# A new opening for a two-layer hybrid block: first shift and scale ahead of x, x in halves, first weights split in slices

## Chip, cores and metric

The kernel runs on one core of one Trainium2 chip. The metric is the device time of one execution in microseconds. Engines are named as in the profile: PE is TensorE, DVE is VectorE, ACT is ScalarE, POOL is GpSimd, SP is SyncE, whose queue issues the transfers (DMAs) here.

## The reference, cut to what matters

Two layers run over 256 latent tokens (x) and 256 context tokens (ctx), 1024 features wide, in fp32. The opening of a layer is a normalisation with a shift and a scale that come from a vector c, followed by one combined input product:

```python
mod = (jax.nn.silu(c) @ w_mod[l] + b_mod[l])[:, None, :]
sh1, sc1, gt1, sh2, sc2, gt2 = jnp.split(mod, N_MOD, axis=-1)
h = rms_norm(x, g_norm1[l]) * (1 + sc1) + sh1      # the same for ctx with c_ctx
z = h @ w_in[l]                                    # 1024 x 4864
# z's columns: conv gates B, C, X (256 each), Fourier F (256), q, k, v, three gates
y_conv = z_B * conv3(z_C * z_X);  y_four = Re(FFT2(z_F));  y_attn = attention(q, k, v)
x = x + gt1 * (gated sum of the three branches @ w_o)
x = x + gt2 * (relu(h2 @ w_ff1) ** 2 @ w_ff2)      # h2: normalised and modulated again
```

The second layer gives the latent tokens only.

## The kernel before

Activations lie feature-major: 128 features of one feature tile on the partitions, 512 tokens (two streams of 256) in the free dimension; there are eight feature tiles (`KT = 8`). For accuracy every product is made of three passes: each operand is split into a high part (`hi`, a rounded copy made by ACT, line 356) and a low part (`lo`, the difference, line 357). In `fm` the passes are lines 416 (high x high), 419 (low weight x high) and 421 (high weight x low activation). A product of one feature tile with the three first weight chunks (F, C, X of `w_in`, 256 columns each) is thus 18 matmuls of 512 columns.

The program is written for a scheduler that orders the instructions of each engine ahead of time by its own model; `tc.keep_in_program_order` pins an instruction behind the one written before it on its engine. Engines then execute their streams strictly in order, and so does SP's queue of transfers. A tile of a pool with n buffers can be written only when the n-th tile before it has been read for the last time. What matters here: `rpool` has two raw weight tiles (1 MB each); the first two weight chunks take both, the third chunk takes the two `modr` tiles, and the next users of the raw tiles are the conv weights (`convL_raw`, columns B of `w_in`) and the Fourier tables (`fouL_raw`).

The opening of layer 0 goes as follows.

- SP issues c and c_ctx, x, ctx (one transfer of 1 MB each), four small row tables (`load_rows`), and then the shift and scale columns of `w_mod` for the eight feature tiles (`start_mod`, line 447, 16 transfers of 512 KB), with the three first weight chunks in two halves of 512 KB each (`start_weights`, line 461), the first halves after the very first `w_mod` part, the second halves after four feature tiles.
- ACT squares x and ctx (line 474), GpSimd raises to the power -1/2 (line 171), VectorE and TensorE spread the result over the partitions (lines 191, 192). TensorE transposes x and ctx (line 480), VectorE and ACT copy the result (line 484).
- For each feature tile, `mod_start` multiplies the `w_mod` columns with silu(c) on TensorE (line 245), VectorE copies the sums (line 252), TensorE turns them (line 254; called the turn of a tile below), VectorE adds the bias (lines 258, 262) and makes the gain (line 231). `modulate` makes the two streams of the tile: VectorE line 209, ACT line 214 (the high part), VectorE line 201 (the low part). The products of the tile before stand around it on TensorE.
- The weight chunks are split in halves of 1024 columns (`Chunk.prep`); of the six low parts four are made by GpSimd (`G`) and two by VectorE.
- Afterwards come the conv stage (products with columns B), Fourier mixing, and q, k, v. Small tables for q and k (`gqk`, `ropec`, `ropes`) are fetched behind the opening's transfers and prepared by VectorE at lines 648 to 654; these instructions are not pinned and the scheduler places them.

Of the kernel before, what the change touches and what calls it, by code (L numbers as in the profile page):

```python
# [15 lines left out]
P = 128  # L16
# [9 lines left out]

# How the streams of work are interleaved in program order.
TAIL = 2                        # low-part passes left for after the next group's start
CT = 4                          # feature tiles of the context's modulation per turn
HEAD = 4                        # feature tiles of stream 0 modulated ahead of stream 1  # L30
NT0 = 2
MLAG = 1                        # tiles between a modulated tile and its split
LAG = 2                         # tiles between a product and its residual
W1, W2 = 3, 2
RATES = [0.6, 1.3, 0.4, 0.8]    # background work emitted per tick
AR = [1.3, 0.8]                 # attention work emitted per tick


@with_exitstack
def hybrid_block_kernel(  # L40
# [30 lines left out]
    def bigt(shape, dt=F32R):  # L71
        return big.tile(shape, dt, tag="big", name=nm("big"))
# [23 lines left out]

# [1 line left out]
    rows = [scratch((P, P)) for _ in range(DEPTH)]  # L98
# [9 lines left out]
    nc.sync.dma_start(crow[8:16, :], c_ctx.rearrange("(a b) -> a b", b=P))  # L108
    xraw = bigt([P, 2, 2, D], F32)
    for i, src in enumerate((x[0], ctx_in[0])):  # L110
        nc.sync.dma_start(xraw[:, i], src.rearrange("(t p) d -> p t d", p=P))
    load_rows(0)

# [30 lines left out]

# [1 line left out]
    xT = const.tile([P, KT, 2 * S], F32, tag="xT", name="xT")  # L146
# [27 lines left out]
    def spread(acc):  # L174
        """1 / rms of each token, on every partition."""
        nt = acc.n // P
        ssp = aux((P, 4))
        for src in (acc.t, acc.q):
            for tt in range(nt):
                PE.matmul(  # L180
                    ssp[:, tt : tt + 1], src[:, tt * P : (tt + 1) * P], ones[:, 0:1],
                    start=src is acc.t and tt == 0, stop=src is acc.q and tt == nt - 1,
                )
        return spread_rows(ssp[:, :nt], nt)[:, : acc.n]
# [38 lines left out]

# [1 line left out]
    modT = [const.tile([P, 48, 2], F32, tag=f"modT{l}", name=f"modT{l}") for l in range(DEPTH)]  # L225
# [11 lines left out]

    def mod_start(ft, parts, meanwhile):
        """Shift and scale of one feature tile, the sums over even and odd k side by side."""
        pb = pmod.tile([P, 2, P], F32, tag="mod", name=nm("mod"))  # L240
        ps, tp = pb[:, 0, :], pb[:, 1, :]
        for kt in range(KT):
            for i in range(2):
                g = 2 * i + kt % 2
                mm = PE.matmul(
                    ps[32 * g : 32 * g + 32, :], cT[:, kt, :], parts[:, i, kt, :],
                    start=kt < 2, stop=kt >= KT - 2,
                )
                if ft and kt == 0 and i == 0:
                    tc.keep_in_program_order(mm)  # L250
        sb = scratch()[:, :P]
        V.tensor_copy(sb, ps)
        meanwhile()
        tc.keep_in_program_order(PE.transpose(tp, sb, ident))
        tv = tp.rearrange("p (g s) -> p g s", s=32)
        for i in (1, 0):
            m = modT[0][:, i * 8 + ft, :]
            V.tensor_tensor(
                m, tv[:, 2 * i, 0:2], prm[0][:, i * 8 + ft : i * 8 + ft + 1].to_broadcast([P, 2]),
                op=ALU.add,  # L260
            )
            V.tensor_tensor(m, tv[:, 2 * i + 1, 0:2], m, op=ALU.add)

# [10 lines left out]
    def mod_finish(accs, dsts, l):  # L274
        """Sum each of two accumulators over the partitions into a column of four features."""
        ps = pmod.tile([P, 256], F32, tag="mod", name=nm("mod"))
# [54 lines left out]

# [1 line left out]
    class Side:  # L333
# [17 lines left out]

# [1 line left out]
    def split(src, n, pin=False, eng=V):  # L353
# [9 lines left out]
    class Chunk:  # L363
# [9 lines left out]
        def at(self, kt, c0, n):  # L373
            hi, lo = self.pieces[kt // 4]
            o = (kt % 4) * 256 + c0
            return hi[:, o : o + n], lo[:, o : o + n]

    def fetch(loads, nkt=8, eng=(V, V)):
        r = raw_tile()
        for dst, src in loads(r.rearrange("p (k n) -> p k n", n=256)):  # L380
            nc.sync.dma_start(dst, src)
        return Chunk([r[:, i * 1024 : (i + 1) * 1024] for i in range(nkt // 4)], eng=eng)
# [10 lines left out]
    def fm(chunks, src, cols, banks=None, kts=range(8), first=None, final=None, pin=False,  # L393
           turn=False, tail=0):
        """Feature-major product. turn: one output tile after the other; tail: so many of the
        last k tiles go chunk after chunk."""
        kts = list(kts)
# [42 lines left out]

# [1 line left out]
    def start_mod(q):  # L442
        t = bigt([P, 2, 2, KT, P], F32)
        for f in range(2):
            for i in (1, 0):
                c0 = i * D + (2 * q + f) * P
                nc.sync.dma_start(  # L447
                    t[:, f, i], w_mod[0, :, c0 : c0 + P].rearrange("(k p) n -> p k n", p=P)
                )
                if (q, f, i) == (0, 0, 0):  # L450
                    start_weights(0)
        return t

# [11 lines left out]

    sc0 = [start_mod(0), start_mod(1)]
    start_weights(1)
    sc0 += [start_mod(2), start_mod(3)]
    first_w = [Chunk(r, True, e) for r, e in zip(start_raw, ((G, V), (G, G), (V, G)))]

# [18 lines left out]

# [1 line left out]
    for l in range(DEPTH):  # L491
# [5 lines left out]

        # modulated norm, Fourier input and the convolution's first factor
        stage[0] = f"n1L{l}"
        sh1 = modT[l][:, 0:8, :]  # L500
        if l == 0:
            hh, hl = bigt([P, KT, 512]), bigt([P, KT, 512])
            gn = None
        else:
            gn = gain(l, 1, 48)
# [4 lines left out]
        if l == 0:  # L510
            banks = [bank() for _ in range(4)] + [aux() for _ in range(2)]

            def go(kt, a=0, b=3):
                fm(first_w[a:b], hsrc, (0, T), banks[2 * a : 2 * b], (kt,), 0, 7, True)

            first_w[0].prep(0)

            def between(kt):
                if kt > 1:
                    go(kt - 1, 0, 1)  # L520
                if kt == KT // 2:
                    first_w[1].prep(1)

            for kt in range(KT):
                mod_start(kt, sc0[kt // 2][:, kt % 2], lambda: between(kt))
                gn = gain(0, 1, 48, gn, kt, 1)
                modulate(hh, hl, [(kt, 0), (kt, 1)], rb, gn, sh1)
                if kt == 0:
                    for w in first_w[1:]:
                        w.prep(0)  # L530
                    turn_x(range(NT0, KT))
                    go(0, 0, 1)
                if kt:
                    go(kt - 1, 1, 3)
                if kt in (2, 4):
                    first_w[kt - 2].prep(1)
            for i in range(3):
                go(KT - 1, i, i + 1)
            mods.set(mod_steps(
                [(0, j, 2) for j in range(2, 6)] + [(1, 1, 2), (1, 0, 2)]  # L540
                + [(1, j, 1) for j in range(2, 6)]
            ), 0.0)
        else:
            banks = fm(first_w, hsrc, (0, T), tail=TAIL)
            banks = banks[2:] + banks[:2]
# [18 lines left out]

        # gated short convolution
        stage[0] = f"convL{l}"
# [34 lines left out]

        # Fourier mixing, over channels
        stage[0] = f"fouL{l}"
# [23 lines left out]

        # Fourier mixing, over positions
        stage[0] = f"fouL{l}"
# [11 lines left out]

        # queries, keys and values, token-major
        stage[0] = f"qkvL{l}"
# [111 lines left out]

        # attention, in steps between the gate products
        ar = Ring(8)
# [64 lines left out]

        # gates and branch projections
        stage[0] = f"gateL{l}"
# [64 lines left out]
        def project(get, src, gt, acc, spreads):  # L889
            """x += gt * (src @ w); the last two chunks go stream by stream when two streams run."""  # L890
            lag = ns == 2 and acc is not None
# [31 lines left out]
        def early(ft):  # L923
            """x times the gain; the product with w_ff1 is divided by the rms instead of x."""
            xf, g = xT[:, ft, :T], gn2[:, ft, 0:1]
# [14 lines left out]

        # MLP
        stage[0] = f"ffL{l}"
# [140 lines left out]
```

## Time and profile before

| | us |
|---|---|
| median of 3 runs | 1157.92 |
| lowest and highest run | 1157.07, 1158.3 |
| span of the profiled execution | 1156.9 |
| busy in it: PE, DVE, ACT, POOL | 1134.0, 781.5, 501.3, 59.3 |

The profile page gives no other time of the profiled execution than its span; the runs shown lie 0.2 to 1.4 us above it. A row of the timeline gives start, duration, engine, line of the kernel, operation, output and inputs, and how often it came in a row; in brackets stands how long the engine had been idle before it and what ended that. Rows that the profile counts as `x2` are two instructions taken together. A matmul's duration overlaps with the next one's, so the pace is read from the starts.

### The profile page before, as it was taken

How to read it: one execution, taken by the hardware profiler on the slowest of the kernel's cores; microseconds unless marked ns; L12 is line 12 of the kernel's file. 1: busy time of each engine (PE TensorE's matmuls, PEld its weight loads, DVE VectorE, ACT ScalarE, POOL GpSimd, SP SyncE). 2: the span in 40 equal slices, each digit the busy share in tenths (PEclk: the TensorE clock that was granted, in tenths of full speed). 3: DMA queues.
4: the chain of work that ended last, by engine and by line, in shares of the span. 5: the costliest groups of instructions: out<-in, count | busy, mean ns of one | idle time of the engine just before them, and what ended most of it. 6: DMA issues, size and time to landing. Idle time of an engine off the chain costs nothing.

```text
span 1156.9 us, 18548 instructions
## 1 busy us (share of the span) xinstructions
PE 1134.0 (98%) x7451; PEld 1001.1 (87%) x7451; DVE 781.5 (68%) x1446; ACT 501.3 (43%) x890; POOL 59.3 (5%) x57
## 2 busy tenths in 40 slices
PE   6899999999999999999999999999999999999998
PEld 4689987887787998878888888899999999999998
DVE  4677775567879785776746664678876567755754
ACT  4244444434332454144234135244666456744641
POOL 2102100000000100000000000043300000000000
PEclk9999999999999999999999999999999999999999
DMA  9923222234656253555455664515434465555552
GB/s 289 288 80 107 92 91 92 83 90 120 192 167 189 77 175 129 185 181 180 134 176 199 212 211 150 188 63 182 129 129 127 123 209 172 197 183 176 189 187 81
DMA packets 165743, 180.06 MB, mean 156 GB/s; under 512 B 5245, under 2 KB 144153, under 8 KB 165657
## 3 DMA queue, kind: packets, MB, share of 16 engines
q1 hardware_dynamic: 165656, 178.88, 49.1%
q8 instruction: 58, 0.95, 0.3%
q14 instruction: 29, 0.23, 0.1%
HBM read 177.81 MB, written 1.05 MB: 155 GB/s over the span
## 4 chain that ended last, share of the span: by engine, by line
PE 90%; SPq 3%; DMA 3%; DVE 2%; ACT 1%; POOL 0%; issue 0%; DVEq 0%; ACTq 0%
PE ffL_mm L416 15%; PE ffL_mm L419 14%; PE ffL_mm L421 14%; PE gateL_mm L416 5%; PE gateL_mm L419 5%; PE gateL_mm L421 5%; PE agL_mm L416 3%; PE agL_mm L419 3%; PE agL_mm L421 3%; SPq L447 2%; PE woL_mm L419 2%; PE woL_mm L421 2%; PE woL_mm L416 2%; PE gateL_aux L796 2%; PE gateL_aux L771 2%; PE qkvL_mm L748 2%
## 5 line engine op out<-in xcount | busy, mean ns | idle before, releaser
L356 ACT CAST ffL_whi<-ffL_raw 128x1024 fp32r<-128x1024 f32 x128 | 134.2, 1050 | 223.5 <-PE ffL_mm L421 211.4
L357 DVE TENSOR_TENSOR ffL_wlo<-ffL_raw,ffL_whi 128x1024 fp32r<-128x1024 f32 x127 | 155.2, 1223 | 102.7 <-ACT ffL_whi L356 102.6
L416 PE MATMUL ffL_mm<-ffL_big,ffL_whi 128*128 128x256 f32 (+1 forms) x544 | 173.3, 329 | 0.3 <-DVE xT L434 0.3
L419 PE MATMUL ffL_mm<-ffL_big,ffL_wlo 128*128 128x256 f32 (+1 forms) x544 | 172.3, 327 | 0.0
L416 PE MATMUL ffL_mm<-woL_big,ffL_whi 128*128 128x258 f32 (+2 forms) x544 | 171.2, 328 | 0.0
L419 PE MATMUL ffL_mm<-woL_big,ffL_wlo 128*128 128x258 f32 (+2 forms) x544 | 170.8, 327 | 0.0
L421 PE MATMUL ffL_mm<-ffL_big,ffL_whi 128*128 128x256 f32 (+1 forms) x544 | 137.9, 327 | 0.0
L421 PE MATMUL ffL_mm<-woL_big,ffL_whi 128*128 128x258 f32 (+2 forms) x544 | 134.0, 328 | 0.0
L416 PEld LDWEIGHTS ffL_mm<-ffL_big,ffL_whi 128*128 128x128 f32 x544 | 103.4, 190 | 11.0 <-issue 2.5
L416 PEld LDWEIGHTS ffL_mm<-woL_big,ffL_whi 128*128 128x128 f32 x544 | 102.7, 189 | 10.2 <-issue 1.6
L419 PEld LDWEIGHTS ffL_mm<-ffL_big,ffL_wlo 128*128 128x128 f32 x544 | 103.4, 190 | 9.0 <-issue 0.4
L419 PEld LDWEIGHTS ffL_mm<-woL_big,ffL_wlo 128*128 128x128 f32 x544 | 102.9, 190 | 8.9 <-issue 0.4
L323 DVE SCALAR_TENSOR_TENSOR ffL_acc<-ffL_modr,cs,ffL_acc 128x512 f32<-128x512 f32 x126 | 90.4, 747 | 25.9 <-DMA ffL_modr<-in_w_mod_dram 24.8
L421 PEld LDWEIGHTS ffL_mm<-ffL_big,ffL_whi 128*128 128x128 f32 x544 | 93.6, 190 | 8.6
L421 PEld LDWEIGHTS ffL_mm<-woL_big,ffL_whi 128*128 128x128 f32 x544 | 91.2, 189 | 8.7
L357 DVE TENSOR_TENSOR gateL_wlo<-gateL_raw,gateL_whi 128x1024 fp32r<-128x1024 f32 x40 | 48.9, 1222 | 13.4 <-ACT gateL_whi L356 13.3
L356 ACT CAST gateL_whi<-gateL_raw 128x1024 fp32r<-128x1024 f32 x40 | 42.0, 1050 | 26.9 <-PE gateL_mm L421 20.7
L774 DVE TENSOR_REDUCE gateL_mx<-gateL_aux 128x1 f32<-128x512 f32 (+1 forms) x48 | 28.7, 600 | 34.5 <-PE gateL_aux L771 34.2
L434 DVE SCALAR_TENSOR_TENSOR xT<-ffL_mm,modT,xT 128x256 f32<-128x256 f32 x80 | 34.1, 478 | 25.3 <-PE ffL_mm L421 25.2
L416 PE MATMUL gateL_mm<-n1L_big,gateL_whi 128*128 128x512 f32 x128 | 50.8, 398 | 0.0
L419 PE MATMUL gateL_mm<-n1L_big,gateL_wlo 128*128 128x512 f32 x128 | 50.8, 397 | 0.0
L419 PE MATMUL woL_mm<-agL_big,woL_wlo 128*128 128x256 f32 (+1 forms) x160 | 47.4, 307 | 0.0
(325 smaller groups left out, 2447.6 us busy)
## 6 DMA issues: line engine op xcount, KB each, us to landing
ffL_raw<-in_w_ff_dram SPq DMA_DIRECT2D x64, 1024.0 KB, 5.2
ffL_modr<-in_w_mod_dram SPq DMA_DIRECT2D x53, 512.0 KB, 5.6
gateL_raw<-in_w_in_dram SPq DMA_DIRECT2D x16, 1024.0 KB, 7.1
init_big<-in_w_mod_dram SPq DMA_DIRECT2D x16, 512.0 KB, 7.6
agL_raw<-in_w_in_dram SPq DMA_DIRECT2D x8, 1024.0 KB, 5.2
woL_raw<-in_w_o_dram SPq DMA_DIRECT2D x8, 1024.0 KB
qkvL_raw<-in_w_in_dram SPq DMA_DIRECT2D x6, 1024.0 KB
agL_modr<-in_w_mod_dram SPq DMA_DIRECT2D x11, 512.0 KB, 3.6
```

Source lines behind the costliest of these rows:

```text
L323: v = V.scalar_tensor_tensor(a, r[:, kk, :], w, a, op0=ALU.mult, op1=ALU.add)
L356: a = A.copy(hi[:, :n], src)
L357: b = eng.tensor_tensor(lo[:, :n], src, hi[:, :n].bitcast(F32), op=ALU.subtract)
L416: m = PE.matmul(d, wh, rh, start=kt == first, stop=False)
L419: PE.matmul(d, wl, rh, start=False, stop=False)
L421: PE.matmul(d, wh, rl, start=False, stop=kt == final)
L434: V.scalar_tensor_tensor(xT[:, f, cs], ps[:, cs], gt[:, f, s : s + 1], xT[:, f, cs], op0=ALU.mult, op1=ALU.add,)
L447: nc.sync.dma_start(t[:, f, i], w_mod[0, :, c0 : c0 + P].rearrange("(k p) n -> p k n", p=P))
L748: PE.matmul(ps, a, wh, start=kt == 0, stop=False)
L771: PE.matmul(sc, qT[:, h, q0 : q0 + P], kT[:, h // 4, e, ks], start=e == 0, stop=e == 1)
L774: V.reduce_max(mx, sc, axis=AX.X, negate=True)
L796: PE.matmul(yp[g * HD : (g + 1) * HD, :], vt[:, k0 + kk, g * HD : (g + 1) * HD], pts[g][:, kk, :], start=kk == 0, stop=kk == nk - 1,)
```

## The change

What it does:

- the `w_mod` columns of feature tile 0 are fetched directly after c, then the row tables, and x and ctx behind them, each in two halves of 512 KB; `mod_start(0)` and its gain stand ahead of the squares;
- `mod_start` takes one or two feature tiles and all its TensorE and VectorE instructions are pinned; tiles 4 and 5 are taken together;
- the first weight chunks (`Sliced`) are split slice by slice: 256 columns of each chunk per feature tile, high part on ACT, low part on VectorE, pinned behind the modulation of the tile; GpSimd makes none;
- the second halves of the weights are fetched after six feature tiles instead of four;
- products come in another order: those of tile 0 with the first two chunks stand ahead of `mod_start(1)`, and for the pair 4 and 5 all products of tile 4 stand ahead of `mod_start(6)`.

```diff
+    def start_mod(t, f):
+        for i in (1, 0):
+            c0 = i * D + f * P
+            nc.sync.dma_start(
+                t[:, f % 2, i], w_mod[0, :, c0 : c0 + P].rearrange("(k p) n -> p k n", p=P)
+            )
+
+    sc0 = [bigt([P, 2, 2, KT, P], F32)]
+    start_mod(sc0[0], 0)
+    load_rows(0)
     for i, src in enumerate((x[0], ctx_in[0])):
-        nc.sync.dma_start(xraw[:, i], src.rearrange("(t p) d -> p t d", p=P))
-    load_rows(0)
+        for tt in range(2):
+            nc.sync.dma_start(xraw[:, i, tt], src[tt * P : (tt + 1) * P, :])
...
-    def mod_start(ft, parts, meanwhile):
+    def mod_start(f0, parts, meanwhile):
+        n = parts.shape[1]
+        pb = pmod.tile([P, 2, n, P], F32, tag="mod", name=nm("mod"))
+        ps, tp = pb[:, 0], pb[:, 1]
         for kt in range(KT):
             for i in range(2):
                 g = 2 * i + kt % 2
+                tc.keep_in_program_order(PE.matmul(
+                    ps[32 * g : 32 * g + 32], cT[:, kt, :], parts[:, :, i, kt, :],
                     start=kt < 2, stop=kt >= KT - 2,
+                ))
+        sb = scratch((P, 4, P))[:, :n]
+        tc.keep_in_program_order(V.tensor_copy(sb, ps))
         meanwhile()
+        for f in range(n):
+            tc.keep_in_program_order(PE.transpose(tp[:, f], sb[:, f], ident))
...
+    class Sliced(Chunk):
+        def part(self, k0, k1):
+            i = k0 // 4
+            if i not in self.pieces:
+                self.pieces[i] = [wpool.tile([P, 1024], F32R, tag=t, name=nm(t))
+                                  for t in ("whi", "wlo")]
+            hi, lo = self.pieces[i]
+            c = slice((k0 - 4 * i) * 256, (k1 - 4 * i) * 256)
+            tc.keep_in_program_order(A.copy(hi[:, c], self.raws[i][:, c]))
+            tc.keep_in_program_order(V.tensor_tensor(
+                lo[:, c], self.raws[i][:, c], hi[:, c].bitcast(F32), op=ALU.subtract))
...
-    sc0 = [start_mod(0), start_mod(1)]
-    start_weights(1)
-    sc0 += [start_mod(2), start_mod(3)]
-    first_w = [Chunk(r, True, e) for r, e in zip(start_raw, ((G, V), (G, G), (V, G)))]
+    start_weights(0)
+    for f in range(1, KT):
+        if f % 2 == 0:
+            sc0.append(bigt([P, 2, 2, KT, P], F32))
+        start_mod(sc0[f // 2], f)
+        if f == 5:
+            start_weights(1)
+    first_w = [Sliced(r) for r in start_raw]
+
+    mod_start(0, sc0[0][:, 0:1], lambda: None)
+    gn = gain(0, 1, 48, None, 0, 1)
...
-            for kt in range(KT):
-                mod_start(kt, sc0[kt // 2][:, kt % 2], lambda: between(kt))
-                gn = gain(0, 1, 48, gn, kt, 1)
-                modulate(hh, hl, [(kt, 0), (kt, 1)], rb, gn, sh1)
...
+            groups = [(0,), (1,), (2,), (3,), (4, 5), (6,), (7,)]
+            due = []
+            for n, fts in enumerate(groups):
+                while len(due) > 1:
+                    go(due.pop(0))
+                f0, nf = fts[0], len(fts)
+                cut = 2 if n == 1 else 1
+                if n == 1:
+                    go(0, 0, 2)
+                if n:
+                    mod_start(f0, sc0[f0 // 2][:, f0 % 2 : f0 % 2 + nf],
+                              lambda: n == 1 or go(due[0], 0, 1))
+                    gn = gain(0, 1, 48, gn, f0, nf)
+                else:
+                    first_w[0].part(0, 1)
+                modulate(hh, hl, [(f, s) for f in fts for s in range(2)], rb, gn, sh1)
+                for w in first_w[not n :]:
+                    w.part(f0, f0 + nf)
+                if n == 0:
                     turn_x(range(NT0, KT))
+                else:
+                    go(due.pop(0), cut, 3)
+                due += fts
             for i in range(3):
                 go(KT - 1, i, i + 1)
```

More of the change, by code (lines that the diff above doesn't have):

```diff
@@ L236, in gain @@
         return g
-    def mod_start(ft, parts, meanwhile):
-        pb = pmod.tile([P, 2, P], F32, tag="mod", name=nm("mod"))
-        ps, tp = pb[:, 0, :], pb[:, 1, :]
+    def mod_start(f0, parts, meanwhile):
+        n = parts.shape[1]
+        pb = pmod.tile([P, 2, n, P], F32, tag="mod", name=nm("mod"))
+        ps, tp = pb[:, 0], pb[:, 1]
         for kt in range(KT):
@@ L244, in mod_start @@
                 g = 2 * i + kt % 2
-                mm = PE.matmul(
-                    ps[32 * g : 32 * g + 32, :], cT[:, kt, :], parts[:, i, kt, :],
+                tc.keep_in_program_order(PE.matmul(
+                    ps[32 * g : 32 * g + 32], cT[:, kt, :], parts[:, :, i, kt, :],
                     start=kt < 2, stop=kt >= KT - 2,
[L248 to L252, printed above, removed]
+                ))
+        sb = scratch((P, 4, P))[:, :n]
+        tc.keep_in_program_order(V.tensor_copy(sb, ps))
         meanwhile()
-        tc.keep_in_program_order(PE.transpose(tp, sb, ident))
-        tv = tp.rearrange("p (g s) -> p g s", s=32)
+        for f in range(n):
+            tc.keep_in_program_order(PE.transpose(tp[:, f], sb[:, f], ident))
+        tv = tp.rearrange("p f (g s) -> p f g s", s=32)
         for i in (1, 0):
-            m = modT[0][:, i * 8 + ft, :]
-            V.tensor_tensor(
-                m, tv[:, 2 * i, 0:2], prm[0][:, i * 8 + ft : i * 8 + ft + 1].to_broadcast([P, 2]),
+            a = i * 8 + f0
+            m = modT[0][:, a : a + n, :]
+            tc.keep_in_program_order(V.tensor_tensor(
+                m, tv[:, :, 2 * i, 0:2], prm[0][:, a : a + n].unsqueeze(2).to_broadcast([P, n, 2]),
                 op=ALU.add,
-            )
-            V.tensor_tensor(m, tv[:, 2 * i + 1, 0:2], m, op=ALU.add)
+            ))
+            tc.keep_in_program_order(
+                V.tensor_tensor(m, tv[:, :, 2 * i + 1, 0:2], m, op=ALU.add))
     def mod_loads(todo):
@@ L376, in at @@
             return hi[:, o : o + n], lo[:, o : o + n]
+    class Sliced(Chunk):
[7 more added lines that the diff above has]
+            tc.keep_in_program_order(A.copy(hi[:, c], self.raws[i][:, c]))
+            tc.keep_in_program_order(V.tensor_tensor(
+                lo[:, c], self.raws[i][:, c], hi[:, c].bitcast(F32), op=ALU.subtract))
     def fetch(loads, nkt=8, eng=(V, V)):
@@ L439, in residual @@
                 acc[s].add(f)
[L442 to L452, printed above, removed]
     start_raw = [raw_tile(), raw_tile()]
@@ L502, in hybrid_block_kernel @@
             hh, hl = bigt([P, KT, 512]), bigt([P, KT, 512])
-            gn = None
         else:
@@ L514, in go @@
                 fm(first_w[a:b], hsrc, (0, T), banks[2 * a : 2 * b], (kt,), 0, 7, True)
[L516 to L522, printed above, removed]
-            for kt in range(KT):
-                mod_start(kt, sc0[kt // 2][:, kt % 2], lambda: between(kt))
-                gn = gain(0, 1, 48, gn, kt, 1)
-                modulate(hh, hl, [(kt, 0), (kt, 1)], rb, gn, sh1)
-                if kt == 0:
-                    for w in first_w[1:]:
-                        w.prep(0)
-                    turn_x(range(NT0, KT))
[L532 to L536, printed above, removed]
+            groups = [(0,), (1,), (2,), (3,), (4, 5), (6,), (7,)]
[17 more added lines that the diff above has]
+                if n == 0:
+                    turn_x(range(NT0, KT))
+                else:
+                    go(due.pop(0), cut, 3)
+                due += fts
             for i in range(3):
```

## The prediction

> **What bounds the kernel now.** I read the page first, then the windows of the opening, then the timeline engine by engine.
>
> ```profile
> span 1156.9 us, 18548 instructions
> ...
> PE   6899999999999999999999999999999999999998
> ...
> PEclk9999999999999999999999999999999999999999
> DMA  9923222234656253555455664515434465555552
> ...
> PE 90%; SPq 3%; DMA 3%; DVE 2%; ACT 1%; POOL 0%; issue 0%; DVEq 0%; ACTq 0%
> ...
> L357 DVE TENSOR_TENSOR ffL_wlo<-ffL_raw,ffL_whi 128x1024 fp32r<-128x1024 f32 x127 | 155.2, 1223 | 102.7 <-ACT ffL_whi L356 102.6
> ```
>
> The chain that ended last is 90% TensorE. Apart from the last slice, only the first two of the 40 have TensorE below 9 and they alone have full transfers, so a change to the opening can win only there. The L357 row prices a whole split on VectorE at 1.22 us. The next view cuts the opening at events used below (us; busy time and count of each engine; granted clock, DMA share, GB/s).
>
> ```profile
> 7.16:20.19 13.03, 9.21 (x74) 7.88 (x74) 6.79 (x20) 8.49 (x16) 3.38 (x2) 1.00 1.11 325
> 20.19:27.87 7.68, 7.17 (x51) 5.07 (x52) 5.53 (x13) 2.74 (x4) 2.37 (x1) 0.78 1.15 292
> 27.87:44.27 16.40, 16.40 (x154) 12.54 (x154) 9.04 (x30) 5.02 (x9) 1.57 (x1) 1.00 1.12 302
> 44.27:54.97 10.70, 7.55 (x53) 5.16 (x52) 7.77 (x26) 1.66 (x3) 3.35 (x2) 0.84 0.94 268
> 54.97:69.66 14.69, 14.69 (x121) 11.73 (x120) 8.09 (x24) 5.39 (x10) 0.27 (x4) 1.00 0.18 62
> 70.00:80.00 10.00, 10.00 (x48) 8.27 (x47) 7.95 (x13) 2.45 (x4) 0.00 (x0) 1.00 0.67 215
> 790.00:795.00 5.00, 3.74 (x32) 3.54 (x31) 5.00 (x11) 2.53 (x4) 0.92 (x2) 1.00 0.65 208
> ```
>
> TensorE idles 3.8 us before 20.19 (13.03 less 9.21) and 3.2 us in 44.27:54.97. After each idle stretch the clock is below 1, which costs (1 - 0.78) x 7.68 = 1.7 us and (1 - 0.84) x 10.70 = 1.7 us: one cold spell is 1.7 us. Between and after, it never idles; the conv stage from 69.66 finds its weights ready. So the measure is when that stage can start, 69.66 now. These rows carry the two stalls and the pace:
>
> ```profile
> 9.93 1.06 ACT L474 ACTIVATE init_junk<-init_big 128x1024 fp32r<-128x1024 f32 x1 [0.60 <-DMA init_big<-in_ctx_dram]
> ...
> 11.93 0.19 ACT L474 ACTIVATION_READ_ACCUMULATOR init_junk<-init_big 128x1 f32 x1
> ...
> 12.59 1.02 POOL L171 TENSOR_TENSOR init_rstd<-init_var,mhalf 128x4 f32<-128x4 f32 x1 [10.78 <-DVE init_var L169]
> ...
> 13.65 0.88 DVE L191 TENSOR_SCALAR init_scr<-ident,init_rstd 128x128 f32<-128x128 f32 x4
> ...
> 18.72 0.87 DVE L209 SCALAR_TENSOR_TENSOR n1L_scr<-xT,n1L_gain,init_aux 128x256 f32<-128x256 f32 x2
> ...
> 20.19 0.80 PE L416 MATMUL n1L_mm<-n1L_big,n1L_whi 128*128 128x512 f32 x1 [2.99 <-ACT n1L_big L214]
> ...
> 24.86 0.33 PE L254 MATMUL n1L_mod<-ident,n1L_scr 128*128 128x128 f32 x1 [0.50 <-DVE n1L_scr L252]
> ...
> 38.80 1.08 PE L245 MATMUL n1L_mod<-init_big,init_scr 128*32 128x128 f32 x32
> ...
> 44.27 1.08 PE L245 MATMUL n1L_mod<-init_big,init_scr 128*32 128x128 f32 x32
> ```
>
> The token scale was worked out from 12.12 to about 14.5, yet the first modulation (L209) waited until 18.72 for the first shift and scale; the first product came 1.47 later. One feature tile takes 5.47 us (38.80 to 44.27): 1.0 for its shift and scale (L245), 0.35 before it, 18 products of 0.23 = 4.1.
>
> ```profile
> 42.70 2.41 POOL L357 TENSOR_TENSOR n1L_wlo<-init_raw,n1L_whi 128x1024 fp32r<-128x1024 f32 x1 [19.18 <-ACT n1L_whi L356]
> ...
> 43.27 4.63 DVE L201 SCALAR_TENSOR_TENSOR n1L_big<-n1L_scr,modT,n1L_big 128x256 fp32r<-128x256 f32 x2 [0.19 <-ACT n1L_big L214]
> ...
> 45.10 2.52 POOL L357 TENSOR_TENSOR n1L_wlo<-init_modr,n1L_whi 128x1024 fp32r<-128x1024 f32 x1
> ...
> 47.95 0.73 PE L421 MATMUL n1L_mm<-n1L_big,n1L_whi 128*128 128x512 f32 x2 [1.48 <-DVE n1L_big L201]
> ...
> 49.26 0.20 DVE L648 TENSOR_SCALAR gqk<-gqk 128x64 f32<-128x64 f32 x1 [1.36 <-DMA gqk<-in_g_q_dram]
> ...
> 50.37 0.33 PE L254 MATMUL n1L_mod<-ident,n1L_scr 128*128 128x128 f32 x1 [1.68 <-DVE n1L_scr L252]
> ```
>
> Two VectorE operations beside GpSimd's split took 4.63 us (0.89 elsewhere, below). Then VectorE waited for the gqk transfer ahead of the copy (L252) that tile 5 needed. Turn (L254) of tile 5 came at 50.37.
>
> **The change, part by part.** Times are of the profiled execution; its span is 1156.9 us, the median 1157.92, so 1.0 us lies around it. What lies after 69.66 is unchanged in work, so I add the shift of that point to the median.
>
> *First shift and scale first, rows ahead of x.* Two more 512 KB transfers (1.05 MB in all) and four small ones go ahead of x on SP's queue. At 302 GB/s (27.87:44.27) the two take 3.5 us, so the last of x and ctx is seen at 9.93 + 3.5 = 13.4. These bytes are moved, not added, so the end of the stream stays.
>
> *x in halves.* Only one square (1.06 + 0.19) then remains, done at 14.7 against 12.12. From there to a possible L209 is about 2.6 us (12.12 to 13.65, four L191, the spread): 17.3, and the first product at 17.4 + 1.47 = 18.9, 1.3 earlier than 20.19. The weights w0, w1, w2 keep their place behind the same bytes. The extra halves cost SP two issues, hidden by the transfers.
>
> *Group 1* issues 12 products ahead of tile 1's shift and scale: 2.7 + 1.35 + 0.7 for copy and signal, turn 1 at 23.7 (24.86 now). TensorE transposes until shortly before 18.9, so I take it as warm.
>
> *Slices.* Per tile VectorE takes three 256-column subtractions more, GpSimd none. Rows:
>
> ```profile
> 62.96 0.27 PE L254 MATMUL n1L_mod<-ident,n1L_scr 128*128 128x128 f32 x1
> ...
> 63.27 0.16 DVE L258 TENSOR_TENSOR modT<-n1L_mod,prm 128x2 f32<-128x2 f32 x1 [1.38 <-PE n1L_mod L254]
> ...
> 63.86 0.88 DVE L209 SCALAR_TENSOR_TENSOR n1L_scr<-xT,n1L_gain,init_aux 128x256 f32<-128x256 f32 x2
> 64.92 0.89 DVE L201 SCALAR_TENSOR_TENSOR n1L_big<-n1L_scr,modT,n1L_big 128x256 fp32r<-128x256 f32 x2 [0.19 <-ACT n1L_big L214]
> ...
> 70.93 0.42 DVE L357 TENSOR_TENSOR fouL_wlo<-fouL_raw,fouL_whi 128x256 fp32r<-128x256 f32 x1
> ```
>
> From a turn to the end of L201 is 2.85 us; three subtractions make it 4.1, then the next copy 0.3. That fits 5.47, so single tiles keep that pace. Turn 2 needs 4.6 (TensorE waits 0.5 for the first slice at 3.3), turn 3 5.5 more: 33.8 (35.85 now). ScalarE's 1.0 us of casts per tile hides in its idle time (5.02 of 16.40 busy).
>
> *Tiles 4 and 5 together.* Their shift and scale takes 2.0 + 0.35 instead of two times 1.35; turn at 33.8 + 6.5 = 40.3. Then VectorE has eight 0.44 operations, ScalarE follows with the cast of 512 columns: the first product of tile 4 can start 4.9 after the turn, its low slice is ready at 5.4. TensorE has only 2.9 us of work: a new stall of 2.4. GpSimd no longer delays anything and the 44.27:54.97 stall goes. VectorE's pinned order runs until about 47; if L648 comes behind it, gqk (seen at 49.26, behind the same bytes) delays no one. Turn 6 is 12.0 later (2.9 + 2.4 + 4.1 + 1.35 + 1.35), 52.3 against 57.49; turn 7 at 57.8 against 62.96. The gain so far is 5.2 us.
>
> *What is late next.* The conv weights reuse the first raw tile. Now its last split starts at 42.70, long before 69.66. With slices its last quarter is subtracted only behind L201 of tile 7, 3.3 us after turn 7, and SP can issue only then. The nearest transfer of this size on a free queue:
>
> ```profile
> 69.89 0.39 PE L416 MATMUL convL_mm<-n1L_big,convL_whi 128*128 128x512 f32 x1
> ...
> 70.45 0.37 SPq L381 DMA_DIRECT2D qkvL_raw<-in_w_in_dram  x1
> ...
> 75.92 1.05 ACT L356 CAST qkvL_whi<-qkvL_raw 128x1024 fp32r<-128x1024 f32 x1 [4.53 <-DMA qkvL_raw<-in_w_in_dram]
> ```
>
> That is 5.5 us to the cast and 1.05 for it: the conv product can start 3.3 + 5.5 + 1.05 = 9.8 after turn 7, at 57.8 + 9.8 = 67.6. TensorE's own work after turn 7 (30 products, 6.8, and 0.5 of waiting for the slice) ends at 7.3: 2.5 us idle where none was. Fourier weights come behind on the same queue and can't fill it. The low part of the conv weights follows 1.2 later (L357); the order of products can hide between all and none of it, and since most products of a half need no low part I take 0.4.
>
> *Cold spells.* Unknown for the idle stretches of 2.4 and 2.5 us. Idle time of 1.26 in 790:795 left the clock at 1.00; 3.2 us in 44.27:54.97 brought 0.84. Each costs 0 to 1.7; between these ends I take half a spell in all, 0.85. [...]
>
> *Sum:* 67.6 + 0.4 + 0.85 = 68.85, 0.8 earlier than 69.66: 1157.92 - 0.8 = **1157.1 us**. Its own range is 1154.9 to 1158.9: with start (1.0), stalls and cold spells at either end.
>
> **Rivals.**
> *A, the pair costs no stall.* If the copy, turns and modulation of tiles 4 and 5 run ahead of TensorE (the pace of a single tile leaves 1.1 us of slack in every round), 2.4 us come back: 1154.7. With a warm conv start too, 1153. Against it: the turns come behind TensorE's own matmuls, so VectorE can't start earlier.
>
> *B, VectorE waits for gqk in the middle of the pair (slower).* L648 is not pinned. Now it stands directly behind tile 4's L201, before the copy for tile 5. If it lands between modulations of the pair, at about 42, VectorE stands until 49.3: 7.3 us, and behind it are the slices that TensorE waits for. 1157.1 + 7.3 = 1164.4. It decides as soon as the wait exceeds about 3 us, which is when L648 stands before 46. For it: the same order of transfers and a wait already there (1.36). Against: VectorE's pinned chain leaves few openings until 47.
>
> *C, both idle stretches bring a cold spell.* 3.4 instead of 0.85: 1159.6, about 0.15% slower. For it: two of the three idle stretches priced above did so.
>
> *D, the opening is bound by its transfers, so that nothing moves.* 0.94 to 1.15 of DMA share until 55 speaks for it; against it, every shift and scale except the first was waiting for its turn on TensorE, not for DMA. It falls in with the first forecast in its time.
>
> **How the numbers follow.** Forecast 0.50 (within it faster 0.17, same 0.27, slower 0.06), A 0.23 (faster), B 0.14 (slower), C with other delays 0.13 (same 0.09, slower 0.04). 0.2% is 2.3 us, about what this measurement can tell from nothing. Faster 0.40, same 0.36, slower 0.24. The range 1152.5 to 1162.5 holds the forecast, A, C and the milder half of B; what is left out is the rest of B and some of A, under 2 in 10.
>
> **What would show it.** Right: the first L416 near 18.9; no DVE row above 1 us beside POOL; L201 pairs at 0.9 throughout; turns at about 23.7, 40.3, 52, 58; an idle row of about 2 us on TensorE in front of tile 4's products, released by ScalarE or VectorE; a conv cast that waits for convL_raw, issued some 3.4 us after the last turn, and 2.5 us idle on TensorE before conv. Wrong: a row of L648 with several us of waiting for gqk before 47 (B); clock below 0.9 in two windows (C); a pair without a stall (A); the conv transfer issued earlier than its last slice.

## The result, and the profile after

The changed kernel takes 1166.74 us (median of 4), the kernel before 1157.57 beside it: ratio 1.0084, 95% interval 1.0072 to 1.0096, slower by 0.84%. The forecast was 1157.1, the range ended at 1162.5. What came is rival B, whose 1164.4 already holds the conv wait of the forecast; the rest is taken up under cold spells below.

The page after; the rows answer to those of before:

```profile
span 1164.6 us, 18508 instructions
...
PE   6799999999999999999999999999999999999998
...
PEclk9899999999999999999999999999999999999999
```

TensorE's second slice has fallen from 8 to 7 and the clock's from 9 to 8; nothing else in the two strips differs. The windows of the changed kernel (us; PE, PEld, DVE, ACT, POOL busy; clock, DMA share, GB/s), cut at its own events:

```profile
19.30:26.00 6.70, 6.28 (x48) 4.78 (x49) 1.72 (x8) 0.55 (x2) 0.00 (x0) 0.75 1.16 291
44.78:53.44 8.66, 0.01 (x2) 0.00 (x1) 4.01 (x20) 1.58 (x4) 0.00 (x0) 0.80 0.60 158
53.44:60.00 6.56, 6.56 (x38) 4.83 (x42) 1.90 (x4) 0.99 (x2) 0.00 (x0) 0.74 0.00 0
...
74.86:80.00 5.14, 2.52 (x7) 1.54 (x7) 5.03 (x8) 3.25 (x4) 0.00 (x0) 0.74 0.72 251
```

There is one stall of 8.66 us with no matmul in it, a second one near 75, and three cold spells where the kernel before had two. The timeline names the two waits (VectorE, then TensorE, then SP's queue and TensorE again; the lines of the changed kernel are L212 for L201, L220 for L209, L265 for L254, L443, L446 and L448 for L416, L419 and L421, L369 and L370 for L356 and L357, L672 for L648, L401 and L402 for the sliced high and low parts):

```profile
41.64 0.38 PE L265 MATMUL n1L_mod<-ident,n1L_scr 128*128 128x128 f32 x2
...
42.65 0.87 DVE L220 SCALAR_TENSOR_TENSOR n1L_scr<-xT,init_gain,init_aux 128x256 f32<-128x256 f32 x2
49.35 0.20 DVE L672 TENSOR_SCALAR gqk<-gqk 128x64 f32<-128x64 f32 x1 [5.83 <-DMA gqk<-in_g_q_dram]
...
50.34 0.47 DVE L212 SCALAR_TENSOR_TENSOR n1L_big<-n1L_scr,modT,n1L_big 128x256 fp32r<-128x256 f32 x1
...
53.44 0.80 PE L443 MATMUL n1L_mm<-n1L_big,n1L_whi 128*128 128x512 f32 x1 [8.65 <-ACT n1L_whi L401]
...
67.45 0.27 PE L265 MATMUL n1L_mod<-ident,n1L_scr 128*128 128x128 f32 x1
...
70.65 0.38 SPq L408 DMA_DIRECT2D convL_raw<-in_w_in_dram  x1
...
77.01 0.99 PE L443 MATMUL convL_mm<-n1L_big,convL_whi 128*128 128x512 f32 x2 [2.15 <-ACT convL_whi L369]
78.48 1.22 PE L446 MATMUL convL_mm<-n1L_big,convL_wlo 128*128 128x512 f32 x2 [0.48 <-DVE convL_wlo L370]
```

After two of the pair's four L220, VectorE's next row is not L212 but L672: it multiplies a small table that has not landed, and stands 5.83 us for it. Everything of the pair is behind it in VectorE's order; ScalarE's casts are behind the pair's last modulation, and TensorE waits for these casts. GpSimd has no row in these windows, and no L212 takes longer than 0.49, so that part does what it says. The conv transfer is issued 3.2 us after the last turn, and TensorE idles 2.15 and 0.48 ahead of conv. In the profiled executions conv starts at 77.01 against 69.89 (the forecast counted from 69.66, 0.2 too early).

### The profile page after: what moved, and what is told of

The parts are those of the page before. It is cut to its first block, busy times and chain, and to the rows that moved or that the text cites. A ratio compares the mean times of both kernels' runs of the same rounds, so it can differ in the third digit from the quotient of the medians.

```text
span 1164.6 us, 18508 instructions
## 1 busy us (share of the span) xinstructions
PE 1135.0 (97%) x7419; PEld 1000.1 (86%) x7419; DVE 780.4 (67%) x1459; ACT 501.7 (43%) x905; POOL 49.4 (4%) x53
## 4 chain that ended last, share of the span: by engine, by line
PE 89%; SPq 3%; DMA 3%; DVE 3%; ACT 1%; issue 1%; POOL 0%; DVEq 0%; ACTq 0%
PE ffL_mm L443 14%; PE ffL_mm L446 14%; PE ffL_mm L448 14%; PE gateL_mm L446 5%; PE gateL_mm L443 5%; PE gateL_mm L448 5%; PE agL_mm L443 3%; PE agL_mm L446 3%; PE agL_mm L448 3%; SPq L114 3%; PE woL_mm L446 2%; PE woL_mm L448 2%; PE woL_mm L443 2%; PE gateL_aux L820 2%; PE gateL_aux L795 2%; PE qkvL_mm L772 2%
## 5 line engine op out<-in xcount | busy, mean ns | idle before, releaser
L369 ACT CAST ffL_whi<-ffL_raw 128x1024 fp32r<-128x1024 f32 x128 | 134.1, 1050 | 224.1 <-PE ffL_mm L448 206.4
L370 DVE TENSOR_TENSOR ffL_wlo<-ffL_raw,ffL_whi 128x1024 fp32r<-128x1024 f32 x127 | 155.2, 1222 | 103.7 <-ACT ffL_whi L369 103.7
L443 PE MATMUL ffL_mm<-ffL_big,ffL_whi 128*128 128x256 f32 (+1 forms) x544 | 173.3, 329 | 0.0
L446 PE MATMUL ffL_mm<-ffL_big,ffL_wlo 128*128 128x256 f32 (+1 forms) x544 | 172.3, 327 | 0.0
L443 PE MATMUL ffL_mm<-woL_big,ffL_whi 128*128 128x258 f32 (+2 forms) x544 | 171.1, 328 | 0.0
L446 PE MATMUL ffL_mm<-woL_big,ffL_wlo 128*128 128x258 f32 (+2 forms) x544 | 170.7, 327 | 0.0
L448 PE MATMUL ffL_mm<-ffL_big,ffL_whi 128*128 128x256 f32 (+1 forms) x544 | 138.0, 327 | 0.0
L448 PE MATMUL ffL_mm<-woL_big,ffL_whi 128*128 128x258 f32 (+2 forms) x544 | 133.9, 328 | 0.0
L443 PEld LDWEIGHTS ffL_mm<-ffL_big,ffL_whi 128*128 128x128 f32 x544 | 103.4, 190 | 10.6 <-issue 2.1
L443 PEld LDWEIGHTS ffL_mm<-woL_big,ffL_whi 128*128 128x128 f32 x544 | 103.0, 190 | 10.2 <-issue 1.6
L446 PEld LDWEIGHTS ffL_mm<-ffL_big,ffL_wlo 128*128 128x128 f32 x544 | 103.5, 190 | 9.1 <-issue 0.4
L446 PEld LDWEIGHTS ffL_mm<-woL_big,ffL_wlo 128*128 128x128 f32 x544 | 103.1, 190 | 8.9 <-issue 0.4
L448 PEld LDWEIGHTS ffL_mm<-ffL_big,ffL_whi 128*128 128x128 f32 x544 | 93.6, 190 | 8.7
L448 PEld LDWEIGHTS ffL_mm<-woL_big,ffL_whi 128*128 128x128 f32 x544 | 91.3, 190 | 8.7
L370 DVE TENSOR_TENSOR gateL_wlo<-gateL_raw,gateL_whi 128x1024 fp32r<-128x1024 f32 x40 | 48.8, 1221 | 14.4 <-ACT gateL_whi L369 14.3
L369 ACT CAST gateL_whi<-gateL_raw 128x1024 fp32r<-128x1024 f32 x40 | 42.0, 1050 | 27.9 <-PE gateL_mm L448 20.7
L443 PE MATMUL gateL_mm<-n1L_big,gateL_whi 128*128 128x512 f32 x128 | 50.8, 398 | 0.0
L446 PE MATMUL gateL_mm<-n1L_big,gateL_wlo 128*128 128x512 f32 x128 | 50.8, 397 | 0.0
L446 PE MATMUL woL_mm<-agL_big,woL_wlo 128*128 128x256 f32 (+1 forms) x160 | 47.4, 307 | 0.0
```

Of the source, the lines that this page charges most:

```text
L369: a = A.copy(hi[:, :n], src)
L370: b = eng.tensor_tensor(lo[:, :n], src, hi[:, :n].bitcast(F32), op=ALU.subtract)
L443: m = PE.matmul(d, wh, rh, start=kt == first, stop=False)
L446: PE.matmul(d, wl, rh, start=False, stop=False)
L448: PE.matmul(d, wh, rl, start=False, stop=kt == final)
```

## Experiments

My theory after the result: two transfers come later than VectorE's fixed order takes for granted (gqk in the pair; the conv weights behind the last slice), and each idle stretch may bring a cold spell. Its rivals: the longer vector chain of pair and slices, the place of the small operations instead of the transfer, and GpSimd. Each ratio is to the kernel before, timed on the same chip.

**Pinning the table preparation.**

```diff
-                V.tensor_scalar(gg, gg, f, None, op0=ALU.mult)
+                tc.keep_in_program_order(V.tensor_scalar(gg, gg, f, None, op0=ALU.mult))
...   # the same for the three products with ropec and ropes
```

> The changed kernel, with the preparation of the q and k tables (L672 to L678, reading gqk) pinned to its written place behind the Fourier stage, in both layers. Theory (VectorE stands in the pair of tiles 4 and 5 until gqk has landed): the products of tile 4 start about 4.9 us after the turn at 41.64, near 46.5 instead of 53.44; 6.9 us come back, 1159.8 us, with 1158 to 1161 as range since a cold spell may stay. Rival (the pair's own longer chain and the slices on VectorE cost the stall, gqk only fills it): little comes back, 1164 or more.

1159.8 us, ratio 1.0029 (1.0019 to 1.0038): 0.55% of 1157, 6.4 us, came back, as the theory said. Turn of the pair, first product of tile 4, last turn, conv, and the windows around conv:

```profile
40.29 0.38 PE L265 MATMUL n1L_mod<-ident,n1L_scr 128*128 128x128 f32 x2
...
45.13 0.50 PE L443 MATMUL n1L_mm<-n1L_big,n1L_whi 128*128 128x512 f32 x1 [1.70 <-ACT n1L_whi L401]
...
57.90 0.27 PE L265 MATMUL n1L_mod<-ident,n1L_scr 128*128 128x128 f32 x1
...
67.48 0.73 PE L443 MATMUL convL_mm<-n1L_big,convL_whi 128*128 128x512 f32 x2 [2.21 <-ACT convL_whi L369]
68.88 1.22 PE L446 MATMUL convL_mm<-n1L_big,convL_wlo 128*128 128x512 f32 x2 [0.67 <-DVE convL_wlo L370]
...
65.00:70.00 5.00, 2.12 (x7) 1.22 (x6) 4.74 (x7) 3.25 (x4) 0.00 (x0) 0.88 0.83 292
70.00:75.00 5.00, 5.00 (x19) 4.01 (x18) 3.91 (x6) 0.00 (x0) 0.00 (x0) 0.78 0.71 214
```

The pair's own stall is the 1.70 us in front of 45.13. With this one wait gone the kernel is still 0.29% slower than before. In its profile conv starts 2.41 us earlier than in the profile before; the 0.67 and the spell behind it (1.7) eat that up, and the spans are 1156.6 and 1156.9. Why the medians lie further apart is taken up under cold spells below.

**Fetching the tables early instead.**

```diff
         start_mod(sc0[f // 2], f)
+        if f == 1:
+            ...   # ropec, ropes, gqk: tiles and the six transfers, moved here
```

> The changed kernel, with the six small transfers for ropec, ropes and gqk issued directly behind the w_mod columns of feature tile 1; nothing is pinned, so L672 to L678 may stand in the middle of the pair. Theory (it is the lateness of the transfer): the stall goes as with pinning, less 0.8 us for 256 KB ahead of the stream and up to 1.5 us of small operations in the chain, 1160 to 1162. Rival (the place of these operations costs, not the transfer): 1165 or more.

1159.94, ratio 1.0030 (1.0017 to 1.0043). The time agrees with the theory, but the run doesn't tell the transfer from the place: with the tables fetched early, the scheduler put all their operations early as well (from the first row on), between 21 and 23 us, before the pair. That it is the transfer rests on the changed kernel's own rows: 5.83 us of waiting ended by the DMA, against about 1.7 us for the 14 operations. The price was another than expected: TensorE waited 3 us for the next w_mod columns, not 0.8.

```profile
21.22 0.19 DVE L673 TENSOR_SCALAR gqk<-gqk 128x64 f32<-128x64 f32 x1 [0.39 <-DMA gqk<-in_g_q_dram]
...
28.89 1.08 PE L257 MATMUL n1L_mod<-init_big,init_scr 128*32 128x128 f32 x32 [2.99 <-DMA init_big<-in_w_mod_dram]
```

**Freeing the conv weights' tile a round earlier**, with the pin and alone.

```diff
                 for w in first_w[not n :]:
-                    w.part(f0, f0 + nf)
+                    if w is not first_w[0] or f0 < 6:
+                        w.part(f0, f0 + nf)
+                    elif f0 == 6:
+                        w.part(6, 8)
```

> As the run with pinned table preparation, and the first chunk's last two slices are split together with tile 6, so its raw tile is free one round (5.4 us) earlier for the conv weights. Theory (the conv stage waits for the raw tile): the idle of 2.15 and 0.48 us on TensorE ahead of the conv products goes, and with it perhaps a cold spell of 1.7: 2.6 to 4.3 us below the run with pinning alone, 1155.5 to 1157.2. Rival (conv weights are bound by the stream of transfers itself): within 0.5 us of the run with pinning alone.

> The changed kernel with only the first chunk's last two slices split with tile 6, so that the conv weights' tile is free a round earlier; table preparation unpinned. Theory (the two new waits stand one behind the other and are independent): the idle ahead of conv and its cold spell go, the wait for gqk stays: 1162 to 1164.5 against 1166.7. Rival (the later wait only makes up for the earlier): no change, 1166 or more.

With the pin: 1153.61, ratio 0.9973 (0.9961 to 0.9984), faster than the kernel before, and 6.2 us below the pin alone, more than the 2.6 to 4.3 expected. The clock accounts for a part: the ten executions of this run had a granted clock of 0.999 on average, those of the pin alone 0.997, a difference of about 2 us in 1155. Alone: 1162.49, ratio 1.0044 (1.0028 to 1.0060), 0.40% below the changed kernel; the pair's stall is still there (first row below, of the run with the tile alone) and conv starts without one (second row). So the two waits stand one behind the other, and each counts.

```profile
52.87 0.79 PE L443 MATMUL n1L_mm<-n1L_big,n1L_whi 128*128 128x512 f32 x1 [9.32 <-ACT n1L_whi L401]
...
74.74 0.39 PE L443 MATMUL convL_mm<-n1L_big,convL_whi 128*128 128x512 f32 x1
```

**Single tiles**, on top of pin and early tile.

```diff
-            groups = [(0,), (1,), (2,), (3,), (4, 5), (6,), (7,)]
+            groups = [(k,) for k in range(KT)]
```

> As the run with pinning and the early last slices, and all eight feature tiles are taken singly instead of 4 and 5 as a pair. Theory (the pair opens a stall of about 2 us because 2.9 us of TensorE work stand against a chain of 4.9): 2 to 3.5 us below the run before it, 1152 to 1155. Rival (the pair saves a turn and a gap, and its stall is hidden): no faster or slower by up to 0.7.

1152.08, ratio 0.9963 (0.9951 to 0.9974). Its turns from the first to the last, in which TensorE has no wait, and conv:

```profile
24.07 0.33 PE L265 MATMUL n1L_mod<-ident,n1L_scr 128*128 128x128 f32 x1 [0.41 <-DVE n1L_scr L262]
28.61 0.27 PE L265 MATMUL n1L_mod<-ident,n1L_scr 128*128 128x128 f32 x1
...
55.88 0.27 PE L265 MATMUL n1L_mod<-ident,n1L_scr 128*128 128x128 f32 x1
...
62.80 0.39 PE L443 MATMUL convL_mm<-n1L_big,convL_whi 128*128 128x512 f32 x1
```

That is 1.5 us less than with the pair, about its stall of 1.70 and less than the 2 to 3.5 expected; the two intervals overlap.

**The same waits in the kernel before.** First the pin alone, then no split on GpSimd alone, then both.

```diff
-    first_w = [Chunk(r, True, e) for r, e in zip(start_raw, ((G, V), (G, G), (V, G)))]
+    first_w = [Chunk(r, True, e) for r, e in zip(start_raw, ((V, V), (V, V), (V, V)))]
```

> The kernel before, with only the preparation of the q and k tables pinned to its written place. Theory (VectorE stood for gqk here too, and GpSimd's split beside it hid a part of that): the wait at 47.9 to 49.26 and the operations behind it go, the turn of tile 5 comes about 2 us earlier and the cold spell of 1.7 may go: 1154 to 1156 against 1157. Rival (the stall between 44 and 51 was GpSimd's alone): within 0.5 us of the kernel before.

> The kernel before, with all six low parts of the first weight chunks made by VectorE and none by GpSimd; the table preparation stays unpinned. Theory (gqk is the later of two waits): VectorE reaches the gqk row earlier and waits longer, the turn of tile 5 comes within 1 us of 50.37, 1156 to 1158. [...]

> The kernel before with both: table preparation pinned and no split on GpSimd. Theory (two waits one behind the other): tiles 4 to 6 keep the pace of 5.5 us, the whole stall of 5.2 us between 44 and 55 goes, 1152 to 1153.5, below either change alone. Rival (the new opening's other parts are needed for it, since VectorE gets 4.9 us more of splits): no better than the better one of the two, 1154 or more.

Pin: 1158.54, ratio 1.0008 (0.9999 to 1.0018). No GpSimd: 1158.70, 1.0017 (1.0008 to 1.0027). Both: 1158.48, 1.0014 (1.0004 to 1.0023). None of the three became faster. The pin lies 2.5 us above its expected range and both edits 5.0 us, and neither rival fits them; without GpSimd the time is 0.7 above its range. Rows 1 and 2 are without GpSimd: VectorE comes early to the gqk row and waits 5.33 instead of 1.36, as expected, and TensorE waits 5.80 for the turn of tile 5 (51.51). Rows 3 and 4 are with the pin alone, rows 5 and 6 with both edits:

```profile
49.11 0.20 DVE L648 TENSOR_SCALAR gqk<-gqk 128x64 f32<-128x64 f32 x1 [5.33 <-DMA gqk<-in_g_q_dram]
...
51.51 0.47 PE L254 MATMUL n1L_mod<-ident,n1L_scr 128*128 128x128 f32 x1 [5.80 <-DVE n1L_scr L252]
...
57.65 1.23 DVE L357 TENSOR_TENSOR convL_wlo<-convL_raw,convL_whi 128x1024 fp32r<-128x1024 f32 x1 [4.94 <-ACT convL_whi L356]
...
59.51 1.08 PE L245 MATMUL n1L_mod<-init_big,init_scr 128*32 128x128 f32 x32 [2.73 <-issue]
...
57.67 1.22 DVE L357 TENSOR_TENSOR convL_wlo<-convL_raw,convL_whi 128x1024 fp32r<-128x1024 f32 x1 [7.36 <-ACT convL_whi L356]
...
59.52 1.94 PE L245 MATMUL n1L_mod<-init_big,init_scr 128*32 128x128 f32 x32 [5.13 <-issue]
```

A third late transfer was next: the split of the conv weights stands in VectorE's order ahead of tile 6's shift and scale, and VectorE waited 7.36 us for it. The pin alone brought the turn of tile 5 to 48.31, two us earlier, as expected, and VectorE then stood 4.94 us at the same place. In the kernel before, the same row began at 57.47, after a wait of only 1.06, because the earlier stall had already used up the time:

```profile
57.47 1.23 DVE L357 TENSOR_TENSOR convL_wlo<-convL_raw,convL_whi 128x1024 fp32r<-128x1024 f32 x1 [1.06 <-ACT convL_whi L356]
```

**Pinning that one as well**, behind tile 7's modulation; then the same with GpSimd's four splits put back.

```diff
             for i in range(3):
                 go(KT - 1, i, i + 1)
+            bch0 = plain(w_in[0], 0, OFF_B)
+            bch0.pin = True
+            bch0.prep(0)
+            bch0.pin = False
...
-        bch = None if last else plain(w_in[l], 0, OFF_B).prep()
+        bch = None if last else bch0.prep()
```

> The kernel before with table preparation pinned, no split on GpSimd, and the split of the conv weights' first half pinned behind tile 7's modulation. In the run without this last pin VectorE stood from 50.3 to 57.67 for the conv weights' transfer, ahead of tile 6's L258. Theory (each late transfer whose consumer stands early in VectorE's order costs a stall; nothing else holds the opening): turns every 5.5 us, conv products from about 63.5, 1152 to 1153.5. Rival (the new opening is needed for the gain): 1155.5 or more.

> The kernel before with both pins (q and k tables, first half of the conv weights) and GpSimd making its four low parts as before. Theory (GpSimd's splits of 1024 columns slow VectorE beside them, and with the two late transfers out of the way nothing hides it): L201 pair of about 4.6 us again, 1.45 us idle on TensorE near 46, 1 to 3 us slower than the same without GpSimd (1152.2): 1153 to 1155. Rival (without the waits GpSimd's work falls beside idle time of VectorE): 1152.2 within 0.6.

Without GpSimd: 1152.19, ratio 0.9962 (0.9951 to 0.9973), the same as the new opening with single tiles (0.9963); conv starts at 63.53. The old opening's order with two pins and no GpSimd is worth as much as the new one. With GpSimd: 1154.82, ratio 0.9986 (0.9976 to 0.9997), 2.6 us slower. The wait of the kernel before is back (rows 2 and 3), and TensorE stands once more, ahead of turn 1 (row 1), where VectorE's own split of 1024 columns took 2.56 us beside GpSimd's (2.55 at 22.06 in the kernel before) instead of 1.22:

```profile
24.32 0.33 PE L254 MATMUL n1L_mod<-ident,n1L_scr 128*128 128x128 f32 x1 [2.02 <-DVE n1L_scr L252]
...
44.31 4.62 DVE L201 SCALAR_TENSOR_TENSOR n1L_big<-n1L_scr,modT,n1L_big 128x256 fp32r<-128x256 f32 x2 [0.19 <-ACT n1L_big L214]
...
48.99 0.50 PE L421 MATMUL n1L_mm<-n1L_big,n1L_whi 128*128 128x512 f32 x1 [1.47 <-DVE n1L_big L201]
```

So taking GpSimd off the splits is worth 2.6 us, but only once nothing later covers it; alone it gained nothing.

**Undoing two more parts** of the new opening in its single-tile version.

```diff
+    for i, src in enumerate((x[0], ctx_in[0])):
+        nc.sync.dma_start(xraw[:, i], src.rearrange("(t p) d -> p t d", p=P))
     start_mod(sc0[0], 0)
     load_rows(0)
-    ...   # x and ctx in halves
```

> The single-tile version with pinned tables and early last slices, with x and ctx as one transfer each again and ahead of tile 0's w_mod columns, all else the same. Theory (the first round is bound by the columns of tile 1, whose bytes lie behind the same sum either way): the first product may come 1 to 2 us earlier, the turn of tile 1 within 0.3 us, the time within 0.5 us of the single-tile version (1152.1). Rival (fetching the first shift and scale ahead of x is what the opening gains by): 1.3 us or more slower.

```diff
-            tc.keep_in_program_order(V.tensor_tensor(
+            tc.keep_in_program_order((G if self is first_w[2] else V).tensor_tensor(
                 lo[:, c], self.raws[i][:, c], hi[:, c].bitcast(F32), op=ALU.subtract))
```

> The single-tile version with pinned tables and early last slices, with the low slices of the third chunk made by GpSimd. Theory (GpSimd's subtractions slow those of VectorE beside them, L201 from 0.45 to 1 us and more, but 1 us per round is free): 0 to 1.5 us slower than 1152.1, rows of VectorE above 0.6 us beside GpSimd. Rival (slices of 256 columns are short enough for no contention to show): VectorE's rows unchanged and the time the same.

x first and whole: 1151.36, ratio 0.9954 (0.9940 to 0.9969), not told apart from the single-tile version; the first product came at 18.54, a microsecond earlier than there (19.63), and turn 1 at 24.55, half a microsecond later than there. That the columns of tile 1 bound this round is not shown: TensorE has no wait for them in either profile, and this execution went through a cold spell in the round, where the single-tile version's had a clock of 1.00:

```profile
18.54:25.00 6.46, 6.03 (x47) 4.33 (x48) 1.52 (x6) 0.55 (x2) 0.00 (x0) 0.74 1.16 290
```

One chunk on GpSimd: 1152.23, ratio 0.9965 (0.9953 to 0.9976), the same; all 16 rows of L212 took 0.48 to 0.49, for GpSimd's slices of 0.79 lay behind these rows, most of them in VectorE's idle time ahead of the next copy. The range of slowing that I expected was therefore not tested by it.

## Why the prediction was wrong

The step that failed is the one sentence on the pair: "VectorE's pinned order runs until about 47; if L648 comes behind it, gqk (seen at 49.26, behind the same bytes) delays no one." It took the row's place in VectorE's order for granted. L672 is not pinned and was put after the pair's second L220, at 43.5. Rival B had the place (between modulations, at about 42), the landing (49.3; measured 49.35) and the price (7.3 us; 6.4 between the ratios with and without the pin). It got 0.14 where its own evidence should have weighed more: the kernel before showed this row in the first moment that VectorE had free behind tile 4, and ScalarE's lag leaves such moments in the pair (0.18 to 0.19 between L209 and L201). "Few openings" was true and beside the point, as one opening is enough.

The rest, by its terms (the pin run shows them without the gqk wait):

| | forecast | changed kernel | with the pin |
|---|---|---|---|
| first product | 18.9 | 19.30 | 19.55 |
| turn of the pair | 40.3 | 41.64 | 40.29 |
| first product of tile 4 | 45.2 | 53.44 | 45.13 |
| turn 7 | 57.8 | 67.45 | 57.90 |
| conv | 67.6 | 77.01 | 67.48 |

- First product (0.7 late), pace of single tiles, the pair's stall (1.70 against 2.4) and the conv wait (2.21 + 0.67 against 2.5 + 0.4) came about as worked out.
- *Cold spells* were mis-sized. I took half a spell for the new stretches and a warm start. In the changed kernel's profile there are three: 0.75 over 6.70, 0.74 over 6.56 and one from 77.01 (0.55 over 2.99 us, then 0.88 over 3.00), 1.7 us each. The start's gap is 1.51 us in seven of the profiles; the clock behind it was 0.75 in the changed kernel (over 6.70 us), 0.72 in the pin with the early tile (20 to 25 us) and 1.00 in the other five (first row below: the pin run; second row: the same run behind its gap of 1.70). So the same gap at the start was followed by a spell in two of these seven executions. The granted clock, measured in every execution of the later runs, averages 0.997 over the ten of the pin run and over the 23 of the kernel before timed beside them. A spell of 1.7 in 1157 is 0.0015, so by estimate both lose two spells, where the forecast counted half a one.

```profile
19.55:25.00 5.45, 5.03 (x49) 3.86 (x50) 2.04 (x11) 0.55 (x2) 0.00 (x0) 1.00 1.16 291
...
45.13:50.00 4.87, 4.65 (x22) 3.34 (x25) 1.87 (x3) 0.99 (x2) 0.00 (x0) 1.00 0.70 176
```

- *The sum without gqk* was 0.8 us faster than before; the pin run is slower by 0.29%, 3.4 us (2.9 between the medians). Between the two profiled executions it is 0.3 faster, near the sum, with one whole spell behind conv (0.88 and 0.78 over 10 us, 1.7 us) for the half. But neither execution was a usual one. The pin run's spans have a median of 1158.0, 1.4 above its profiled one, whose clock was 0.999. The 23 spans of the kernel before timed beside it have a median of 1155.1, 1.8 below the profiled 1156.9 from which I counted. What made that execution slower was not measured. Rival C, at 1159.6, has the pin run's time (1159.8) but not its mechanism: in the profile a spell came only behind the conv wait (0.78), not behind the pair's stall (1.00), so the match in the number is luck.
- *What brings a spell* is not shown. The gap of 1.70 in the pin run (43.42 to 45.13) was followed by a clock of 1.00. Behind 2.73 us (pin in the kernel before, 59.51) the 32 rows of L245 took 1.08 us, as at 38.80 in the kernel before, in a stretch at 1.00; behind 5.13 us (pin and no GpSimd there, 59.52) they took 1.94. The 1.51 us at the start was followed by 0.75 and 0.72 in two executions and by 1.00 in five, the 2.21 and 0.67 ahead of conv by 0.78. So the length of the gap alone did not decide it in these executions.
- *GpSimd.* The forecast credited the change with the whole old stall because GpSimd left. The experiments show it was two stalls on top of each other, of which GpSimd's was the shorter: without GpSimd TensorE still waited 5.80 us, with the two late rows pinned it waited 1.47 at this place.

## What to carry to other kernels

When engine orders are fixed ahead of time, look for each instruction that reads a transfer, ask when its bytes really land in the queue's order, and what stands behind it on its engine; pin it behind the work that must not wait, or expect a faster stage to run into it (here 5.33 us for the table without GpSimd, where the kernel before waited 1.36). Here a stall that ended with two causes close together, the late table and GpSimd's splits, went away only with both, and the next late transfer took its place: VectorE then waited 7.36 us for the conv weights. In the kernel before, two late transfers and GpSimd's splits had to be out of the way before the opening gave 0.4%. When a buffer is consumed in slices, ask when its last slice is read: here SP issued the next transfer into it 3.2 us after the last turn (70.65), and with the last two slices taken a round earlier 1.85 us ahead of that turn (57.33 against 59.18, pin with the early tile).

## What the runs showed of the hardware that I had not expected

Six small transfers, 256 KB in all, put into the stream ahead of the columns of tile 2 made TensorE wait 3.0 us for these columns, where the run with the pin has no such wait; at the stream's 291 GB/s their bytes are worth 0.9. Their six issue rows on SP's queue took 0.43 to 2.84 us in this run, 5.1 in sum, and the stream then carried 232 GB/s (below), where the pin run has 291 over nearly the same stage. Why small transfers cost that much is not shown.

```profile
19.70:25.00 5.30, 4.89 (x48) 3.71 (x49) 3.60 (x23) 0.54 (x2) 0.00 (x0) 1.00 0.89 232
```
